# Attention with all products on 128 rows of weights, both parts of V side by side, in a hybrid encoder kernel

## The chip, the cores and the metric

The kernel runs on one core of one Trainium2 chip. The metric is device time in microseconds (us) of one execution; lower is better. The time before is the median of three runs, 1886.88 us (1886.74 to 1887.07).

## The reference, cut to what matters

The program is a two-layer encoder on 512 tokens of width 1024. Layer 0 has a pooling and state-space mixer, layer 1 has the attention that the change is about. The tokens form a grid of 8 rows by 64 columns; each of 16 heads (64 channels) lets a token see all 8 rows and 16 columns around its own.

```python
def neighborhood_attention(h, w_qkv, rpb, w_out):
    qkv = (h @ w_qkv).reshape(bsz, rows, GRID_W, 3, N_HEADS, HEAD_DIM)
    q = qkv[:, :, :, 0] * (HEAD_DIM ** -0.5)
    k = qkv[:, :, :, 1]
    v = qkv[:, :, :, 2]
    ...
    s = jnp.einsum('bqhd,biqjhd->bhqij', q_r, k_nb).astype(F32) + bias[None]
    p = jax.nn.softmax(s.reshape(bsz, N_HEADS, GRID_W, kh * KW), axis=-1)
    ...
    return jnp.einsum('bhqij,biqjhd->bqhd', p, v_nb)
    ...
    return o @ w_out

for layer in range(DEPTH):
    h = h + 0.5 * rms_norm(swiglu_ffn(rms_norm(h, g[0]), ...), g[1])
    h = h + rms_norm(mixer_or_attention(rms_norm(h, g[2])), g[3])
    h = h + 0.5 * rms_norm(swiglu_ffn(rms_norm(h, g[4]), ...), g[5])
```

## The kernel before

**Split numbers.** Each operand of a large product is stored as two parts, hi (its value in the 4-byte type fp32r) and lo (the rest). ScalarE writes hi by a copy, VectorE or GpSimd writes lo by a subtraction (`split_evac`, L391 to L405). A full product is three products in one sum: hi by hi, hi by lo, lo by hi (`mm3`, L179 to L183). Most lines of TensorE in the trace are therefore L181, L182 and L183; which product it is shows in the names of the tiles.

**The attention** (L766 to L981). Queries and keys are ordered by columns, so that a query tile of 128 tokens (16 columns by 8 rows) needs one contiguous set of 192 or 256 keys. A *unit* is one head and one of its four query tiles: 16 heads by 4 tiles are 64 units. Heads come in pairs `hp`; the two heads of a pair, `a` = 0 and 1, have their channels on partitions 0 to 63 and 64 to 127 of the projections' output.

- `evac_q` and `evac_k` (L786 to L805) split a pair's Q and K. Per head, tile `q0` or `q1` holds hi of the scaled Q on the head's own 64 partitions and lo on the other 64; tile `k0` or `k1` holds hi of K on both halves (L805 copies it across). One tile `k_lo` holds lo of K for both heads, each on its own half.
- `scores(u)` (L890): two products into the only bank `ps_qk`. L898 uses all 128 rows (hi and lo of Q against hi of K), L899 uses the head's 64 rows (hi of Q against lo of K). Then VectorE adds the bias, takes the row's extreme and writes `p` (L902), and ScalarE takes exp (L904).
- `normalize(u)` (L909): reciprocal and product on VectorE, L912 and L914.
- `transpose(u)` (L916): TensorE turns `p` (L922), and a split makes `pt_hi` and `pt_lo` (ScalarE L396, VectorE L397). For tiles 0 and 3 one of the two chunks has only 64 keys.
- `values(u)` (L931): per unit two chunks of keys, each an `mm3` of V's parts against the parts of P, 64 columns of weights and 128 columns moving. For tiles 0 and 3 one of the chunks has 64 rows. After tile 3 the 64x512 result is split into `oT`.

**What sets the order.** Each engine runs its instructions in the order in which the code issues them. The loop over `slot` (L946) runs the units in a software pipeline: in slot s stand the deferred VectorE work (`run_later`), normalize of unit s-1, values of unit s-5, transpose of unit s-3, scores of unit s, one step of `run_spread` (the splits of a new pair's Q and K), and 1.35 *fill steps* on average (`FILL_RATE`): pieces of the projections of V, Q and K of later heads, and in the last slots of the output projection. A fill step is six products of 512 columns or twelve of 256 (three of 512 in the output projection). After the loop the rest of the output projection runs, and the norm behind it uses `gpost`, a row of gains spread over all partitions.

Weights come by DMA from SyncE's queue (`w_raw`, two buffers). ScalarE makes `w_hi` (L124), and inside the loop GpSimd makes `w_lo` (L135). The same DMA queue brings the bias, 512 KB per head, two heads ahead, and `gpost`, which is loaded ahead of the attention (L769).

## Time and profile before

| | us |
|---|---|
| median of three runs | 1886.88 |
| the profiled execution, span of its instructions | 1884.6 |
| the profiled execution, its device time | 1886.41 |
| TensorE (PE) busy in the span | 1831.5 (97%) |
| weight loads (PEld) | 1639.3 (87%) |
| VectorE (DVE) | 1470.7 (78%) |
| ScalarE (ACT) | 925.7 (49%) |
| GpSimd (POOL) | 350.4 (19%) |
| the attention's loop, first to last score product | 1292.4 to 1485.1 |

The times of the timeline are counted from the span's start. A matmul's row has the time at which it starts and how long it is in the array; matmuls overlap, so that the distance between two starts, not the duration, is what one costs in a stream. The form `64*128 64x192` means weights of 64 rows by 128 columns, and an output of 192 columns; `128*64` has 128 rows and 64 columns. A wait names the engine that waits, the tile and line, and after the arrow what ended the wait; then the sum in us, how many times, and the longest.

### The profile page before, as it was taken

How to read it: one execution, taken by the hardware profiler on the slowest of the kernel's cores; microseconds unless marked ns; L12 is line 12 of the kernel's file. 1: busy time of each engine (PE TensorE's matmuls, PEld its weight loads, DVE VectorE, ACT ScalarE, POOL GpSimd, SP SyncE). 2: the span in 40 equal slices, each digit the busy share in tenths (PEclk: the TensorE clock that was granted, in tenths of full speed). 3: DMA queues.
4: the chain of work that ended last, by engine and by line, in shares of the span. 5: the costliest groups of instructions: out<-in, count | busy, mean ns of one | idle time of the engine just before them, and what ended most of it. 6: DMA issues, size and time to landing. Idle time of an engine off the chain costs nothing.

```text
span 1884.6 us, 31563 instructions
## 1 busy us (share of the span) xinstructions
PE 1831.5 (97%) x12368; PEld 1639.3 (87%) x12368; DVE 1470.7 (78%) x2380; ACT 925.7 (49%) x1749; POOL 350.4 (19%) x238
## 2 busy tenths in 40 slices
PE   7999999998899999999999999999999999999998
PEld 7887987787689999988999998888878789999886
DVE  6888989868779999844899996465565589999744
ACT  5254446354455444543644445355555465444532
POOL 2021322015011233200122320012222012322100
PEclk9999999999999999999999999999999999999999
DMA  6474346647432333332233324323222132333321
GB/s 196 128 224 165 110 137 194 202 132 256 161 125 79 101 112 102 107 107 78 94 109 102 103 89 135 101 80 122 90 93 99 62 106 96 102 106 102 123 96 62
DMA packets 82021, 225.48 MB, mean 120 GB/s; under 512 B 15792, under 2 KB 20048, under 8 KB 80848
## 3 DMA queue, kind: packets, MB, share of 16 engines
q1 hardware_dynamic: 70176, 197.80, 31.8%
q0 software_dynamic: 6960, 23.57, 4.1%
q10 hardware_dynamic: 4736, 2.10, 0.4%
q8 instruction: 97, 1.59, 0.4%
q14 instruction: 52, 0.43, 0.1%
HBM read 206.69 MB, written 18.84 MB: 120 GB/s over the span
## 4 chain that ended last, share of the span: by engine, by line
PE 62%; DVE 7%; ACT 3%; issue 1%; DMA 1%; DVEq 0%; ACTq 0%
PE ps_gu L183 10%; PE ps_gu L182 10%; PE ps_gu L181 10%; PE ps_A L183 3%; PE ps_A L182 3%; PE ps_A L181 3%; PE ps_B L182 3%; PE ps_B L181 3%; PE ps_B L183 3%; PE ps_f L181 3%; PE ps_f L182 2%; PE ps_f L183 2%; DVE w_lo L135 1%; PE ps_qk L899 1%; ACT junk L237 1%
## 5 line engine op out<-in xcount | busy, mean ns | idle before, releaser
L135 DVE TENSOR_TENSOR w_lo<-w_raw,w_hi 128x1024 fp32r<-128x1024 f32 x214 | 283.3, 1329 | 215.8 <-ACT w_hi L124 215.6
L124 ACT CAST w_hi<-w_raw 128x1024 fp32r<-128x1024 f32 (+1 forms) x313 | 262.9, 864 | 286.4 <-PE ps_A L183 71.3
L183 PE MATMUL ps_gu<-xT_hi,w_lo 128*128 128x256 f32 (+1 forms) x1008 | 307.5, 305 | 2.5 <-DVE w_lo L135 2.5
L183 PE MATMUL ps_gu<-xsum,w_lo 128*128 128x256 f32 x1088 | 308.2, 283 | 0.6 <-DVE w_lo L135 0.6
L182 PE MATMUL ps_gu<-xsum,w_hi 128*128 128x256 f32 x1088 | 307.8, 283 | 0.2 <-DVE xsum L518 0.2
L181 PE MATMUL ps_gu<-xsum,w_hi 128*128 128x256 f32 x1088 | 307.6, 283 | 0.0
L181 PE MATMUL ps_gu<-xT_hi,w_hi 128*128 128x256 f32 (+1 forms) x1008 | 304.9, 302 | 0.0
L182 PE MATMUL ps_gu<-xT_lo,w_hi 128*128 128x256 f32 (+1 forms) x1008 | 304.5, 302 | 0.0
L183 PEld LDWEIGHTS ps_gu<-xsum,w_lo 128*128 128x128 f32 x1088 | 208.6, 192 | 0.9 <-DVE w_lo L135 0.8
L182 PEld LDWEIGHTS ps_gu<-xsum,w_hi 128*128 128x128 f32 x1088 | 208.5, 192 | 0.4 <-DVE xsum L518 0.4
L181 PEld LDWEIGHTS ps_gu<-xsum,w_hi 128*128 128x128 f32 x1088 | 208.4, 192 | 0.0
L183 PEld LDWEIGHTS ps_gu<-xT_hi,w_lo 128*128 128x128 f32 x1008 | 190.4, 189 | 15.0 <-DVE w_lo L135 4.1
L181 PEld LDWEIGHTS ps_gu<-xT_hi,w_hi 128*128 128x128 f32 x1008 | 190.2, 189 | 8.5 <-issue 0.9
L182 PEld LDWEIGHTS ps_gu<-xT_lo,w_hi 128*128 128x128 f32 x1008 | 190.2, 189 | 7.3
L135 POOL TENSOR_TENSOR w_lo<-w_raw,w_hi 128x1024 fp32r<-128x1024 f32 x31 | 74.1, 2390 | 562.2 <-ACT w_hi L124 532.1
L109 POOL TENSOR_TENSOR w_u<-w_raw,w_s 128x512 f32<-128x512 f32 x64 | 112.2, 1754 | 354.9 <-ACT w_hi L124 196.3
L124 ACT CAST w_hi<-w_s 128x512 fp32r<-128x512 f32 x136 | 77.8, 622 | 197.3 <-DVE w_s L105 193.5
L105 DVE TENSOR_TENSOR w_s<-w_raw,w_u 128x1024 f32<-128x1024 f32 x68 | 145.8, 2144 | 2.3
L640 POOL TENSOR_TENSOR g<-g,m 128x1024 f32<-128x1024 f32 x34 | 94.6, 2782 | 244.9 <-DVE m L638 244.9
L181 PE MATMUL ps_B<-w_hi,gT 128*128 128x512 f32 x352 | 137.1, 389 | 1.6 <-DVE free L1264 1.6
L183 PE MATMUL ps_A<-w_hi,gT 128*128 128x512 f32 x352 | 137.1, 389 | 1.1 <-DVE gT L693 1.1
L181 PE MATMUL ps_A<-w_hi,gT 128*128 128x512 f32 x352 | 137.3, 390 | 0.0
(376 smaller groups left out, 4251.2 us busy)
## 6 DMA issues: line engine op xcount, KB each, us to landing
w_raw<-in_w_gu_dram SPq DMA_DIRECT2D x106, 512.0 KB, 3.4
w_raw<-in_w_dn_dram SPq DMA_DIRECT2D x88, 512.0 KB, 3.3
w_u<-in_w_gu_dram SPq DMA_DIRECT2D x70, 512.0 KB, 3.7
w_raw<-in_w_qk_dram SPq DMA_DIRECT2D x16, 512.0 KB, 3.3
bias<-in_att_bias_dram SPq DMA_DIRECT2D x16, 512.0 KB, 4.1
w_raw<-in_w_in_dram SPq DMA_DIRECT2D x8, 512.0 KB, 3.3
cm<-m_dram SPq DMA_DIRECT2D x4, 1024.0 KB, 8.7
w_raw<-in_w_ao_dram SPq DMA_DIRECT2D x8, 512.0 KB, 3.9
```

What stands on the lines that cost most here:

```text
L105: tt(out=blocks(s), in0=g[:, :HALF].unsqueeze(1).broadcast_to([P, 2, HALF]), in1=blocks(u)[:, :2], op=ALU.subtract)
L109: (h_engine or self.nc.gpsimd).tensor_tensor(out=z["h"], in0=g[:, HALF:], in1=z["s"][:, HALF:], op=ALU.add)
L124: self.nc.scalar.copy(hi[:, k:k + step], src[:, k:k + step])
L135: (engine or self.lo_engine).tensor_tensor(out=lo[:, :n], in0=src, in1=hi[:, :n].bitcast(F32), op=ALU.subtract)
L181: mm(ps, a[0], b[0], start=start, stop=False)
L182: mm(ps, a[0], b[1], start=False, stop=False)
L183: mm(ps, a[1], b[0], start=False, stop=stop)
L237: self.nc.scalar.activation(out=junk[:, :src.shape[-1]], in_=src, func=AF.Square, scale=scale, accum_out=out)
L640: nc.gpsimd.tensor_tensor(out=rows(f), in0=rows(f), in1=m, op=ALU.mult)
L899: nc.tensor.matmul(ps[:, :n], tq[rows], lo[rows], start=False, stop=True)
```

## The change

- **Scores.** K's lo gets the layout of its hi: a tile per head with lo on both halves. ScalarE's copy of hi across stays, and GpSimd copies lo across (`nc.gpsimd.tensor_copy`). Both products now use 128 rows. Lo of the second head of a pair lives in the buffer that `gpost` had; `gpost` is loaded after the loop.
- **V** is stored with hi and lo of a head side by side, 128 columns of weights: the upper 64 rows of the result are the sum with hi, the lower 64 the sum with lo.
- **P** lies in one buffer of eight chunks per part, four tiles by two; the unused halves of chunks 0 and 7 are zero, written once.
- **values** works after tiles 1 and 3 only. Two neighbouring chunks of two query tiles that need the same 128 keys are one product of 256 columns. After tile 3 ScalarE copies the lower half of the result out (`o_sum`), VectorE adds the upper half in the next slot, and the split follows one slot later than that. `run_later` runs what was there when it began, and a call made by it waits for the next slot.
- **Bias** is loaded per unit, four units ahead, in four buffers; `p` has four buffers where it had five.
- **After the loop** the output projection of token tile 3 starts with its first two weight tiles, and the last products of tiles 0 to 2 come behind them.
- **Elsewhere** a small constant of the mixer in layer 0, `edge`, is loaded in the mixer and not at the program's start.

```diff
         def run_later():
-            while later:
-                later.pop(0)()
+            now = later[:]
+            del later[:]
+            for f in now:
+                f()
...
-        def load_bias(head):
-            bias[head] = z["ap"].tile([P, 4, 256], F32, tag="bias", bufs=2, name="bias")
-            nc.sync.dma_start(bias[head], ins["att_bias"][head])
+        def load_bias(u):
+            if u < 64:
+                n = self.NKEY[u % 4]
+                bias[u] = z["ap"].tile([P, 256], F32, tag="bias", bufs=4, name="bias")[:, :n]
+                nc.sync.dma_start(bias[u], ins["att_bias"][u // 4, :, u % 4, :n])
...
         def evac_k(hp, ps):
-            k[hp] = [z["ap"].tile([P, SEQ], F32R, tag="k" + n, bufs=2, name="k" + n) for n in ("0", "1", "_lo")]
-            for a, x in enumerate(k[hp][:2]):
+            hi = [z["ap"].tile([P, SEQ], F32R, tag="k%d" % a, bufs=2, name="k%d" % a) for a in range(2)]
+            lo = [z["ap"].tile([P, SEQ], F32R, tag="k_lo", bufs=2, name="k_lo"), z["k_lo"][:, hp % 2]]
+            k[hp] = list(zip(hi, lo))
+            for a, x in enumerate(k[hp]):
                 own, other = own_other(a)
-                lo = []
-                self.split_evac(x[own], k[hp][2][own], ps[own], None, lo)
+                rest = []
+                self.split_evac(x[0][own], x[1][own], ps[own], None, rest)
                 yield
-                lo[0]()
-                nc.scalar.copy(x[other], x[own].bitcast(F32))
+                rest[0]()
+                nc.scalar.copy(x[0][other], x[0][own].bitcast(F32))
+                nc.gpsimd.tensor_copy(x[1][other], x[1][own].bitcast(F32))
...
-        vt = [ap.tile([P, TT, D], F32R, name=n) for n in ("v_hi", "v_lo")]
+        vt = ap.tile([P, TT, 16, 2, 64], F32R, name="v")
+        pt = [ap.tile([P, 8, P], F32R, name="pt" + n) for n in ("_hi", "_lo")]
+        for x in pt:
+            nc.scalar.mul(x[:64, 0], self.ident[:64], 0.0)
+            nc.scalar.mul(x[64:, 7], self.ident[64:], 0.0)
...
-            nc.tensor.matmul(ps[:, :n], tq, hi, start=True, stop=False)
-            nc.tensor.matmul(ps[:, :n], tq[rows], lo[rows], start=False, stop=True)
+            for i, x in enumerate(k[hp][a]):
+                nc.tensor.matmul(ps[:, :n], q[hp][a][:, t * P:(t + 1) * P], x[:, self.KEY0[t]:self.KEY0[t] + n],
+                                 start=i == 0, stop=i == 1)
...
         def values(u):
...
-            for c, (_, n, s, r) in enumerate(self.CHUNKS[t]):
-                self.mm3(o[:64, t * P:(t + 1) * P], [x[r:r + n, s, d0:d0 + 64] for x in vt],
-                         [x[r:r + n, c] for x in pt], c == 0, c == 1)
-            if t == 3:
-                hi, lo = (x[64 * a:64 * a + 64, hp, :].rearrange("p (r c) -> p r c", r=8) for x in oT)
-                self.split_evac(hi, lo, o[:64].rearrange("p (c r) -> p r c", r=8), None, later)
...
+            def product(s, *chunks):
+                n = len(chunks) * P
+                at = chunks[0] // 2 * P
+                for i, x in enumerate(pt):
+                    nc.tensor.matmul(o[:, at:at + n], head[:, s],
+                                     x[:, chunks[0]:chunks[-1] + 1].rearrange("p c n -> p (c n)"),
+                                     start=s == 1 and i == 0, stop=chunks[-1] == 7 and i == 1)
+            if t == 1:
+                product(1, 1, 2)
+                product(0, 0)
+                return
+            product(3, 5, 6)
+            product(2, 3, 4)
+            product(0, 7)
...
+            w = ap.tile([P, SEQ], F32, tag="o", bufs=1, name="o_sum")[64 * a:64 * a + 64]
+            nc.scalar.copy(w, o[64:])
+            def rest():
+                V.tensor_tensor(out=w, in0=o[:64], in1=w, op=ALU.add)
+                self.split_evac(hi, lo, by_row(w), None, later)
+            later.append(rest)
...
-        run_later()
+        while later:
+            run_later()
+        self.load_gpost(1, 3)
...
-        for _ in out_steps((0, 1, 2), (KT - 1,)):
-            pass
-        self.post_pair(0, 0, psA)
         for kt in range(KT):
             for _ in out_steps((3,), (kt,)):
                 pass
+            if kt == 1:
+                for _ in out_steps((0, 1, 2), (KT - 1,)):
+                    pass
+                self.post_pair(0, 0, psA)
```

On TensorE, near the loop's end: the last values of a slot, the two transposes and the scores of a 256-key unit before the change. `ps_o` is the result of the values, `ps_pt` the turned P, `ps_f` a fill product; the shape behind a name is that of the output.

```order
L181 MATMUL ps_o<-pt_hi,v_hi 64x128
L182 MATMUL ps_o<-pt_lo,v_hi 64x128
L183 MATMUL ps_o<-pt_hi,v_lo 64x128
L922 MATMUL ps_pt<-ident,p 128x128
L922 MATMUL ps_pt<-ident,p 64x128
L898 MATMUL ps_qk<-k_15462,q_15348 128x256
L899 MATMUL ps_qk<-k_lo,q_15348 128x256
L181 MATMUL ps_f<-w_hi,oT_hi 128x512
```

The same place after it, in the slot of the values of tile 1.

```order
L958 MATMUL ps_o<-pt_hi,v 128x256
L958 MATMUL ps_o<-pt_lo,v 128x256
L958 MATMUL ps_o<-pt_hi,v 128x128
L958 MATMUL ps_o<-pt_lo,v 128x128
L934 MATMUL ps_pt<-ident,p 128x128
L934 MATMUL ps_pt<-ident,p 64x128
L911 MATMUL ps_qk<-k_15324,q_15215 128x256
L911 MATMUL ps_qk<-k_lo,q_15215 128x256
L181 MATMUL ps_f<-w_hi,oT_hi 128x512
```

The values went from 24 products a head, of 64x128 each, to 10 of 128 output rows; the transposes and the number of score products stayed.

On VectorE, where a head ends in the last slots, before: two ISA rows are the reduction L902 and its accumulator.

```order
L902 ISA p,att_m<-ps_qk,bias 128x192
L902 ISA att_m 128x1
L397 TENSOR_TENSOR oT_lo<-ps_o,oT_hi 64x512
L397 TENSOR_TENSOR pt_lo<-ps_pt,pt_hi 128x256
L912 RECIPROCAL att_r<-att_s 128x1
L914 TENSOR_SCALAR p<-p,att_r 128x192
L902 ISA p,att_m<-ps_qk,bias 128x256
```

And after: the reduction is L915, reciprocal and product L924 and L926.

```order
L975 TENSOR_TENSOR o_sum<-ps_o,o_sum 64x512
L397 TENSOR_TENSOR pt_lo<-ps_pt,pt_hi 128x256
L924 RECIPROCAL att_r<-att_s 128x1
L926 TENSOR_SCALAR p<-p,att_r 128x192
L915 ISA p,att_m<-ps_qk,bias 128x256
L915 ISA att_m 128x1
L397 TENSOR_TENSOR oT_lo<-o_sum,oT_hi 64x512
```

The addition `o_sum` took the place of `oT_lo`, and `oT_lo` moved behind the next reduction.

On GpSimd, the last weights of the loop before:

```order
L135 TENSOR_TENSOR w_lo_15101<-w_raw_14848,w_hi_15100 128x1024
L135 TENSOR_TENSOR w_lo_15210<-w_raw_14963,w_hi_15209 128x1024
L135 TENSOR_TENSOR w_lo_15351<-w_raw_15104,w_hi_15350 128x1024
L135 TENSOR_TENSOR w_lo_15466<-w_raw_15213,w_hi_15465 128x1024
L135 TENSOR_TENSOR w_lo_16088<-w_raw_15928,w_hi_16087 128x1024
```

and after, the copies for the last pair of heads:

```order
L135 TENSOR_TENSOR w_lo_15218<-w_raw_14992,w_hi_15217 128x1024
L135 TENSOR_TENSOR w_lo_15328<-w_raw_15093,w_hi_15327 128x1024
L811 CAST k_lo_15325<-k_lo_15325 64x512
L811 CAST k_lo_13017<-k_lo_13017 64x512
L135 TENSOR_TENSOR w_lo_15902<-w_raw_15742,w_hi_15901 128x1024
```

Two copies of lo of K now stand on GpSimd for each pair, behind a `w_lo`.

## Rows read from the trace of the kernel before

**Rows 1.** The page: span, and the granted clock of TensorE in 40 slices.
```profile
span 1884.6 us, 31563 instructions
...
PEclk9999999999999999999999999999999999999999
```

**Rows 2.** Busy time by stretch in us, instructions in brackets; granted clock, DMA.
```profile
core 0: us, PE busy (x) PEld busy (x) DVE busy (x) ACT busy (x) POOL busy (x), PEclk, DMA share, GB/s
...
1350.00:1400.00 50.00, 50.00 (x331) 40.64 (x330) 29.86 (x97) 30.09 (x79) 12.02 (x6) 1.00 0.28 95
...
1470.00:1493.00 23.00, 23.00 (x152) 17.64 (x151) 13.71 (x52) 10.41 (x35) 0.00 (x0) 1.00 0.13 46
```

**Rows 3.** Waits of VectorE in the loop, 1292 to 1494 us.
```profile
DVE p L902 <- PE ps_qk L899: 53.4, 48, 2.7
DVE att_r L912 <- ACT p L904: 11.1, 25, 1.9
```

**Rows 4.** Timeline of TensorE at unit 0 (192 keys): start us, us.
```profile
1292.39 0.25 PE L898 MATMUL ps_qk<-k,q 128*128 128x192 f32 x1
1292.57 0.35 PE L899 MATMUL ps_qk<-k_lo,q 64*128 64x192 f32 x1
1292.86 0.38 PE L181 MATMUL ps_f<-w_hi,xT_hi 128*128 128x256 f32 x1
1293.08 0.28 PE L182 MATMUL ps_f<-w_lo,xT_hi 128*128 128x256 f32 x1
```

**Rows 5.** The same view at unit 2 (256 keys).
```profile
1297.88 0.38 PE L899 MATMUL ps_qk<-k_lo,q 64*128 64x256 f32 x1
...
1298.42 0.28 PE L182 MATMUL ps_f<-w_lo,xT_hi 128*128 128x256 f32 x1
1298.54 0.28 PE L183 MATMUL ps_f<-w_hi,xT_lo 128*128 128x256 f32 x1
```

**Rows 6.** The same view at the values of a tile 3.
```profile
1354.60 0.28 PE L183 MATMUL ps_f<-w_hi,xT_lo 128*128 128x256 f32 x1
1354.71 0.22 PE L181 MATMUL ps_o<-pt_hi,v_hi 128*64 128x128 f32 x1
...
1354.84 0.22 PE L183 MATMUL ps_o<-pt_hi,v_lo 128*64 128x128 f32 x1
1354.99 0.27 PE L181 MATMUL ps_o<-pt_hi,v_hi 64*64 64x128 f32 x1
1355.10 0.22 PE L182 MATMUL ps_o<-pt_lo,v_hi 64*64 64x128 f32 x1
...
1355.31 0.44 PE L922 MATMUL ps_pt<-ident,p 128*128 128x128 f32 x2
```

**Rows 7.** Timeline of the weight loads behind unit 0's scores.
```profile
1292.86 0.19 PEld L181 LDWEIGHTS ps_f<-w_hi,xT_hi 128*128 128x128 f32 x1
1292.96 0.19 PEld L182 LDWEIGHTS ps_f<-w_lo,xT_hi 128*128 128x128 f32 x1
1293.08 0.19 PEld L183 LDWEIGHTS ps_f<-w_hi,xT_lo 128*128 128x128 f32 x1
```

**Rows 8.** VectorE's groups in the loop: count, busy us, mean ns, idle before.
```profile
L397 DVE TENSOR_TENSOR oT_lo<-ps_o,oT_hi 64x512 fp32r<-64x512 f32 x16 | 10.9, 682 | 2.7 <-ACT oT_hi L396 2.4
```

**Rows 9.** Line L914 alone: duration in ns, least, median, longest.
```profile
L914 DVE TENSOR_SCALAR p<-p,att_r x64: 319/353/1124, 1296.6 to 1486.8; 128x192 f32<-128x192 f32 x32, 128x256 f32<-128x256 f32 x32
```

**Rows 10.** GpSimd's groups in the whole span: count, busy us, mean ns, idle before.
```profile
L135 POOL TENSOR_TENSOR w_lo<-w_raw,w_hi 128x1024 fp32r<-128x1024 f32 x31 | 74.1, 2390 | 562.2 <-ACT w_hi L124 532.1 <-PE ps_pt L922 20.8 <-PE ps_qk L899 9.3
...
L1485 POOL TENSOR_TENSOR pz<-pz 128x543 f32<-128x543 f32 x4 | 4.4, 1092 | 34.2 <-ACT pz L1479 34.2
```

**Rows 11.** Timeline at unit 56, the first of the last pair of heads.
```profile
1467.00 2.38 POOL L135 TENSOR_TENSOR w_lo<-w_raw,w_hi 128x1024 fp32r<-128x1024 f32 x1 [7.47 <-ACT w_hi L124]
...
1467.22 0.68 DVE L397 TENSOR_TENSOR k_lo<-ps_f,k 64x512 fp32r<-64x512 f32 x1
...
1468.64 0.35 PE L898 MATMUL ps_qk<-k,q 128*128 128x192 f32 x1
```

**Rows 12.** DMA issues: count, KB each, median us from issue to landing.
```profile
bias<-in_att_bias_dram SPq DMA_DIRECT2D x16, 512.0 KB, 4.1
...
gpost<-in_norm_g_dram SPq DMA_DIRECT2D x6, 512.0 KB, 5.6
```

More of the change, by code (lines that the diff above doesn't have):

```diff
@@ L812, in start @@
             z["ap"] = tc.alloc_tile_pool(name="attn", bufs=1)
-            load_bias(0)
-            load_bias(1)
+            z["k_lo"] = self.base.tile([P, 2, SEQ], F32R, tag="gpost", bufs=1, name="k_lo")
+            for u in range(4):
+                load_bias(u)
         def evac_first(i, ps):
@@ L847, in v_steps @@
             for b, ps in enumerate(pv):
-                hi, lo = (x[:, 2 * b:2 * b + 2, c * 256:(c + 1) * 256] for x in vt)
-                self.split_evac(hi, lo, ps.rearrange("p (s n) -> p s n", s=2), None, later)
+                hi, lo = (vt[:, 2 * b:2 * b + 2, 4 * c:4 * c + 4, i] for i in range(2))
+                self.split_evac(hi, lo, ps.rearrange("p (s h d) -> p s h d", s=2, h=4), None, later)
             self.W.done()
@@ L891, in scores @@
             hp, a, t = u // 8, u // 4 % 2, u % 4
-            rows, n = slice(64 * a, 64 * a + 64), self.NKEY[t]
+            n = self.NKEY[t]
             ps = self.bank("ps_qk")
@@ L905, in scores @@
             st[u] = p, s
-            if t == 3 and 2 * hp + a + 2 < 16:
-                load_bias(2 * hp + a + 2)
+            load_bias(u + 4)
         def normalize(u):
@@ L916, in transpose @@
         def transpose(u):
-            p, _ = st[u]
+            p, _ = st.pop(u)
             ps = self.bank("ps_pt")
-            pt = [ap.tile([P, 2, P], F32R, tag="pt" + n, bufs=2, name="pt" + n) for n in ("_hi", "_lo")]
-            ch = self.CHUNKS[u % 4]
+            t = u % 4
+            ch = self.CHUNKS[t]
             for c, (o, n, _, _) in enumerate(ch):
@@ L923, in transpose @@
             if ch[0][1] == ch[1][1]:
-                self.split_evac(pt[0], pt[1], ps[:, :256].rearrange("p (c n) -> p c n", c=2), None, later)
+                self.split_evac(*(x[:, 2 * t:2 * t + 2] for x in pt),
+                                ps[:, :256].rearrange("p (c n) -> p c n", c=2), None, later)
             else:
                 for c, (_, n, _, r) in enumerate(ch):
-                    self.split_evac(pt[0][r:r + n, c], pt[1][r:r + n, c], ps[:n, c * P:(c + 1) * P],
-                                    None, later)
@@ L929, in transpose @@
-            st[u] = pt
+                    self.split_evac(*(x[r:r + n, 2 * t + c] for x in pt), ps[:n, c * P:(c + 1) * P], None, later)
         def values(u):
             hp, a, t = u // 8, u // 4 % 2, u % 4
-            if t == 0:
-                st["o"] = self.bank("ps_o")
-            o = st["o"]
-            pt = st.pop(u)
-            d0 = (2 * hp + a) * 64
-            for c, (_, n, s, r) in enumerate(self.CHUNKS[t]):
-                self.mm3(o[:64, t * P:(t + 1) * P], [x[r:r + n, s, d0:d0 + 64] for x in vt],
-                         [x[r:r + n, c] for x in pt], c == 0, c == 1)
@@ L941, in values @@
-            if t == 3:
-                hi, lo = (x[64 * a:64 * a + 64, hp, :].rearrange("p (r c) -> p r c", r=8) for x in oT)
-                self.split_evac(hi, lo, o[:64].rearrange("p (c r) -> p r c", r=8), None, later)
+            if t == 1:
+                o = st["o"] = self.bank("ps_o")
+            elif t == 3:
+                o = st.pop("o")
+            else:
+                return
+            head = vt[:, :, 2 * hp + a].rearrange("p s i d -> p s (i d)")
+            def product(s, *chunks):
[5 more added lines that the diff above has]
+                                     start=s == 1 and i == 0, stop=chunks[-1] == 7 and i == 1)
@@ L1339, in mixer @@
         xh, xl = self.xT
-        edge, scol, bcol = self.mix_small
+        scol, bcol = self.mix_small
         con = {}
@@ L1356, in start @@
         def start():
-            nonlocal yp, y, yhl, sp, us
+            nonlocal yp, y, yhl, sp, us, edge
             yp = tc.alloc_tile_pool(name="mix_y", bufs=1)
@@ L1361, in start @@
             sp = tc.alloc_tile_pool(name="mix", bufs=1)
+            edge = sp.tile([P, 4, 16], F32, name="edge")
+            G.dma_start(edge, ins["pool_edge"].partition_broadcast(P))
             us = sp.tile([P, 32, 64], F32, name="us")
@@ L1666, in build @@
             self.mix_small = [self.base.tile([P, *n], F32, name="mix_" + k)
-                              for k, *n in (("edge", 4, 16), ("scol", 4), ("bcol", 4))]
+                              for k, *n in (("scol", 4), ("bcol", 4))]
             self.h = self.base.tile([P, TT, D], F32, name="h")
@@ L1687, in first_norm @@
         step(1)
[L1688 to L1689 removed]
+        scol, bcol = self.mix_small
         nc.gpsimd.dma_start(scol, self.ins["pool_sc"])
```

15 lines of the change are left out of this document (7 added, 8 removed).

## The prediction

> **What bounds the kernel now.** I read the page first, then the stretches of the attention, then who waits in it, and last the order of TensorE's starts. The granted clock is full in all 40 slices [rows 1], so no time hides in the clock. In the loop TensorE is busy in all of 50 us and all of 23 us of two stretches, while VectorE and ScalarE have 30 of 50 us and GpSimd 12 [rows 2]. VectorE waits for the score products, 53.4 us in 48 of the 64 units [rows 3]; TensorE hardly waits for it. So here the time is the sum of the distances between TensorE's starts, and I priced the change in these distances.
>
> In a stream with equal shapes, 256 columns come every 0.11 to 0.12 us [rows 4 to 6]; I take 0.117. Products of 128 columns on 64 columns of weights come every 0.06 us (0.13 for two steps) [rows 6]. A change between 128 and 64 rows breaks the stream. Of a 192-key unit without transposes ahead of it, L898 starts at 1292.39, L899 0.18 later, the next fill product 0.29 after that, and the one behind it 0.22 later [rows 4]: 0.69 us from L898 to the second fill product. In the values of tile 3 the step to 64 rows is 0.15 us in place of 0.06, the next 0.11, and the step back to the transposes 0.15 [rows 6].
>
> **The change part by part.**
>
> *Scores.* With 128 rows throughout, the same distance would be two score products and one fill product. A product of 192 columns would be about 0.09 by its columns, but loads of 128 columns of weights start no closer than 0.10 to 0.12 (0.22 for two) [rows 7], so 0.11. That is 0.11 + 0.11 + 0.117 = 0.34, and 0.35 saved. With 256 keys, L899 to the second fill product is 0.54 against 0.51 [rows 4, 5]; L898 to L899, which in rows 5 includes a wait, I take as 0.18 + 0.03. That is 0.75 against 0.35, and 0.40 saved. 32 x 0.35 + 32 x 0.40 = 24.0 us. By 0.09 for 192 columns it is 1.3 us more, by 0.12 for everything about 1 us less.
>
> *Values.* Tile 3 takes 0.71 us from the last fill product to the transposes, less that product's own step of 0.117: 0.59 [rows 6]. Tile 0 has the same two changes of rows, 0.59. Tiles 1 and 2 take 6 x 0.06 = 0.36 each. A head costs 1.90 us. After it, a head has six products of 256 columns and four of 128, all on 128 columns of weights: 6 x 0.117, and for the small ones between 0.06 (what they cost now on 64 columns) and 0.117; I take the load's 0.11 [rows 7]. That is 1.14 us, and 0.76 saved; 16 heads give 12.2 us, with ends at 11.7 and 15.4. Both parts together: 36.2 us off TensorE in the loop, 0.57 a unit.
>
> [...] The rows show loads of 128 rows that start 0.11 us apart with 0.19 us each [rows 7], under products of 128 rows. [...]
>
> *VectorE.* Per head one more operation of 64x512: `oT_lo` from PSUM takes 0.68 us now [rows 8]; the addition `o_sum` reads PSUM too and I give it the same, with `oT_lo` in SBUF no cheaper. 16 x 0.68 = 10.9 us, 0.17 a unit. ScalarE gets 16 more copies of that size behind VectorE's addition; it has 20 us free in 50 [rows 2], so no cost, and if that cover were gone exp would come later by a copy.
>
> *What of it VectorE gives back.* It is the next bound: only one bank holds scores, so TensorE can't write unit u+1 before L902 has read unit u. The 53.4 us that it waits for TensorE [rows 3] shrink by 36.2 and by 10.9, and 6.3 us are left. Over the whole loop it would just do, but the slack is uneven: in 64 - 48 = 16 units L902 finds its scores ready, VectorE is late already, and what is taken off TensorE there it can't use. That is at most 16 x (0.57 + 0.17) = 11.8 us, and at least 0, when the next longer slot makes up for it. I take 8, nearer the upper end: the late units stand at the heads' and pairs' starts, where the splits of Q and K pile up (unit 56 in [rows 11]), and a late unit passes its delay on.
>
> *GpSimd.* 16 copies of 64x512, of which four lie ahead of the loop. No such copy is in the trace; the nearest rows are an addition of 128x543 at 1.09 us and `w_lo` of 128x1024 at 2.39, half of which is 1.2 [rows 10]. I take 1.1, with ends at half of the first row, 0.5, and at the whole of the second, 2.39. Each stands behind a `w_lo` in GpSimd's queue. By the count of fill steps a pair's K is split in slots 12, 18, 30, 36, 42 and 54 for first use in 16, 24, 32, 40, 48 and 56: four slots or six ahead, but two for pairs 4 and 7. For pair 7 `w_lo` runs from 1467.00 to 1469.38, and unit 56 starts at 1468.64 [rows 11]: its second product would wait until about 1470.5, 2 us; but VectorE is late there by nearly as much, so 0.5 counts, and as much for pair 4. Further, L914 takes 0.35 us alone and up to 1.12 beside GpSimd [rows 9]; 12 copies cost VectorE at most 12 x 0.77 = 9.2 us, and I count 0.7 of it as seen by TensorE. Together 1.7 us, between 0 and 6.
>
> *Edits with no cost.* The zeros of P are four small operations ahead of the first V projection, in which ScalarE has time. `gpost` lands in 5.6 us [rows 12]; it is issued after the last scores, and five slots and some products lie ahead of its first use, so it is hidden; without them the norm waits up to 5.6 us. The bias is now 64 loads of a quarter of the size, each waiting on SyncE's queue for L902 of its unit; behind it wait weight loads, which have two buffers and four split tiles ahead. A whole head's bias lands in 4.1 us [rows 12], and four slots of some 2.6 us are its lead; if a weight load in front of it waits for a `w_lo` (2.39), the lead still holds. After the loop the chain from the last value to `oT_lo` grows from two operations to four, about 1.3 us more; two weight tiles of token tile 3, six products of 512 columns, each two steps of 0.117, or 1.4 us, now stand in front. Without them the wait is 1.1 us. The `edge` load leaves the start and goes to GpSimd's queue in the mixer, where GpSimd waits 34.2 us for its first work [rows 10]. All zero, with 1 us to either side.
>
> *Sum.* 36.2 - 8 - 1.7 = 26.5 us. The profiled execution has a span of 1884.6 [rows 1] and took 1886.41, within 0.5 of the median of 1886.88; I take the gain off the median: 1860.4, so 1860.
>
> **The rivals.**
> - *VectorE doesn't hold TensorE back.* For it: 53.4 us of waiting exceeds 47.1 of new demand. Against it: the 16 late units. Then 36.2 us go, 1850.7; with the cheaper ends of the products 1849.
> - *The chain of VectorE and ScalarE takes over.* If `L914` and the new `oT_lo`, whose two operands are in SBUF, run beside GpSimd often, demand is 36.2 + 10.9 + 9.2 = 56.3, 2.9 above the 53.4; with all of 11.8 for uneven slots and 3 for the copies TensorE gives back 17.7. The gain is 18.5 and the time 1868.
> - *The pauses don't come from the change of rows*, and each load waits anyway. Scores save nothing; a head's values cost 6 x (0.11 + 0.117) + 4 x (0.11 + 0.06) = 2.04 against 1.90, and the time is 1886.9 + 2 = 1889. [...] Against it: the value products of tiles 1 and 2 have the same operands as those of 0 and 3 and no pause.
> - *Slower: the scores wait for GpSimd's copies.* The second product of the first unit of each head needs a copy that stands behind a `w_lo`: 2.39 + 1.09 = 3.5 us for each of the 12 copies in the loop is 42 us, against 36.2 - 8 saved: 1886.9 + 14 = 1901. It turns to slower when a copy costs more than 28/12 = 2.4 us. Against it: four of six pairs have 4 slots or more to spare.
>
> **How the numbers follow.** The forecast, a gain between 21 and 33 us, has 0.66; no holding back 0.10; the chain of VectorE and ScalarE 0.15; pauses that stay 0.04; slower by the copies 0.05. The time is 1860, with its own range 1853 to 1866. The range 1849 to 1872 takes in the second case and the third to a gain of 15 us and leaves out the last two and the tails, about 0.2. A measurement of this kernel can tell 0.2%, 3.8 us, from no change: faster 0.66 + 0.10 + 0.15 = 0.91; the case of the pauses gives the same, 0.04; slower 0.05.
>
> **What would show it.** Right: the two products L911 start 0.11 to 0.12 apart, with no longer step behind them; a head's values are ten products with 1.1 to 1.2 us of steps; the loop is about 26 us shorter; VectorE's wait for scores falls from 53 to some 15 us, and TensorE has waits for `att_m` of about 8 us that it lacks now; GpSimd's copies take about 1.1 us. Wrong: steps of 0.18 to 0.3 us that remain around L911; waits of L911 for GpSimd at more pairs than two; waits for the bias or `gpost`; or TensorE with 15 us and more of waits in the loop.

## The result, and the profile after

The changed kernel takes 1860.04 us (median of four runs, 1858.23 to 1861.25), beside 1886.81 for the kernel before in the same comparison: a ratio of 0.9857, with a 95% interval of 0.984 to 0.9874. The forecast was 1860, with a range of 1849 to 1872. The total was right, but some of its terms were off and made up for each other; most of what follows is about that.

The profiled execution took 1858.23 us. First the page's span and busy times (share of the span, count), to be read against [rows 1]:

```profile
span 1856.5 us, 31301 instructions
PE 1796.5 (97%) x12144; PEld 1623.3 (87%) x12144; DVE 1491.7 (80%) x2396; ACT 944.5 (51%) x1769; POOL 360.7 (19%) x254
```

"Loop" below is the time from the start of the first score product to the start of the last one.

| us | before | after | change |
|---|---|---|---|
| ahead of the loop | 1292.4 | 1288.2 | -4.2 |
| loop | 192.75 | 169.32 | -23.4 |
| behind it | 399.5 | 399.0 | -0.5 |
| span | 1884.6 | 1856.5 | -28.1 |

Of the 4.2 us ahead of the loop 1.7 are the clock: from 20 us on, the sum of (1 - granted clock), explained below, is 6.8 us there before and 5.1 after. In the other runs it lies between 5.1 and 12.0, though what runs there is nearly the same program; so one fall of the clock more or less need not come from an edit.

**TensorE's steps.** The timeline of TensorE in the changed kernel (start, duration, operation; weights' rows x columns, then the output), at unit 0 with 192 keys and at the values of a tile 1:

```profile
1288.22 0.26 PE L911 MATMUL ps_qk<-k,q 128*128 128x192 f32 x1
1288.31 0.28 PE L911 MATMUL ps_qk<-k_lo,q 128*128 128x192 f32 x1
1288.43 0.30 PE L181 MATMUL ps_f<-w_hi,xT_hi 128*128 128x256 f32 x1
1288.56 0.28 PE L182 MATMUL ps_f<-w_lo,xT_hi 128*128 128x256 f32 x1
...
1339.10 0.28 PE L958 MATMUL ps_o<-pt_lo,v 128*128 128x256 f32 x1
1339.21 0.22 PE L958 MATMUL ps_o<-pt_hi,v 128*128 128x128 f32 x1
1339.28 0.28 PE L958 MATMUL ps_o<-pt_lo,v 128*128 128x128 f32 x1
1339.39 0.41 PE L934 MATMUL ps_pt<-ident,p 128*128 128x128 f32 x2
```

From the first score product to the second fill product it is 0.34 us, where [rows 4] had 0.69: the long steps behind the 64-row product are gone. Of two value products of 128 columns the first is followed by the second after 0.06 to 0.07 us, not after the 0.11 that the forecast took; behind the second, where a transpose follows, it is 0.11.

**Waits in the loop** (engine, tile and line <- what ended the wait: us in total, times, longest), after:

```profile
DVE p L915 <- PE ps_qk L911: 13.8, 19, 2.3
PEld ps_qk L911 <- DVE att_m L915: 7.4, 9, 2.3
PEld ps_qk L911 <- POOL k_lo L811: 2.4, 2, 1.3
PEld ps_qk L911 <- ACT k L810: 1.9, 1, 1.9
```

The same rows of TensorE before, which did not stand ahead:

```profile
PEld ps_qk L898 <- DVE att_m L902: 1.1, 2, 1.0
PEld ps_qk L898 <- ACT k L805: 0.2, 1, 0.2
```

VectorE's wait for scores fell from 53.4 [rows 3] to 13.8 us. TensorE's weight loads for the scores wait 11.7 us in place of 1.3 (its products wait in the same gaps, and are not counted again). The longest waits stand ahead of unit 2 (1.4, and 1.0 before), unit 17 (2.3), unit 41 (1.0), the second product of unit 32 (1.2), and both products of unit 56 (1.9 and 1.3).

**The clock.** The stretches of 1 us behind the wait of unit 17 (busy time of PE, PEld, DVE, ACT, POOL with counts, then the granted clock, the DMA share, GB/s), and TensorE's products there:

```profile
1333.00:1334.00 1.00, 0.00 (x0) 0.00 (x0) 0.82 (x2) 0.12 (x1) 0.98 (x1) 1.00 0.00 0
1334.00:1335.00 1.00, 0.70 (x3) 0.62 (x4) 1.00 (x4) 0.66 (x3) 0.00 (x0) 0.85 0.11 12
1335.00:1336.00 1.00, 1.00 (x4) 0.81 (x3) 0.90 (x5) 1.00 (x1) 0.00 (x0) 0.50 0.89 242
1336.00:1337.00 1.00, 1.00 (x4) 0.81 (x3) 0.97 (x1) 0.87 (x3) 0.00 (x0) 0.50 0.93 355
1337.00:1338.00 1.00, 1.00 (x4) 0.72 (x4) 0.88 (x4) 0.00 (x0) 0.00 (x0) 0.50 0.46 136
1338.00:1339.00 1.00, 1.00 (x6) 0.83 (x5) 0.00 (x0) 0.00 (x0) 0.00 (x0) 0.94 0.03 9
```

```profile
1334.30 0.39 PE L911 MATMUL ps_qk<-k,q 128*128 128x256 f32 x1 [2.10 <-DVE att_m L915]
...
1336.29 0.63 PE L182 MATMUL ps_f<-xT_lo,w_hi 128*128 128x512 f32 x1
1336.71 0.63 PE L183 MATMUL ps_f<-xT_hi,w_lo 128*128 128x512 f32 x1
...
1338.28 0.39 PE L181 MATMUL ps_f<-xT_hi,w_hi 128*128 128x512 f32 x1
1338.51 0.40 PE L182 MATMUL ps_f<-xT_lo,w_hi 128*128 128x512 f32 x1
```

Right behind a wait of 2.3 us the granted clock of TensorE was 0.50, and products of 512 columns came every 0.42 us in place of 0.23. The same happens from 1444.0 on, behind the waits of unit 56. Before, the loop has no such stretch; over the whole of it the granted clock is 1.00:

```profile
1292.00:1485.00 193.00, 192.25 (x1223) 154.06 (x1221) 115.79 (x388) 111.84 (x295) 47.85 (x20) 1.00 0.28 95
```

What the clock took is the sum of (1 - granted clock) over stretches of 1 us, 1.7 us for each of the two, 3.4 together.

So a loop splits into waits, clock, and the rest, which I call steps: before 1.3 + 0 + 191.4, after 11.7 + 3.4 + 154.2. TensorE's steps are 37.2 us shorter, and 13.8 us of that went back: 10.4 to waits, 3.4 to the clock. There is one trace of each kernel, so a single fall of the clock, 1.7 us of loop, may come and go without any edit; where a reading below hangs on one, the text says so.

### The profile page after: what moved, and what is told of

It is laid out like the page before. It is cut to its first block, busy times and chain, and to the rows that moved or that the text cites. A ratio compares the mean times of both kernels' runs of the same rounds, so it can differ in the third digit from the quotient of the medians.

```text
span 1856.5 us, 31301 instructions
## 1 busy us (share of the span) xinstructions
PE 1796.5 (97%) x12144; PEld 1623.3 (87%) x12144; DVE 1491.7 (80%) x2396; ACT 944.5 (51%) x1769; POOL 360.7 (19%) x254
## 4 chain that ended last, share of the span: by engine, by line
PE 58%; DVE 9%; ACT 4%; issue 2%; DMA 1%; POOL 0%; DVEq 0%; ACTq 0%; POOLq 0%
PE ps_gu L183 10%; PE ps_gu L182 10%; PE ps_gu L181 10%; PE ps_A L181 3%; PE ps_A L183 3%; PE ps_A L182 3%; PE ps_B L183 3%; PE ps_B L182 3%; PE ps_B L181 3%; PE ps_f L181 2%; PE ps_f L183 2%; DVE w_lo L135 2%; PE ps_f L182 2%; ACT junk L237 1%; DVE xsum L518 1%
```

## The experiments

All runs in one table, split in the same way (us; waits are those of the weight loads for scores). The last column is the ratio of the time to the kernel before, whose median lay between 1884.8 and 1886.8 in these comparisons; so runs are compared by ratio or by loop.

| run | loop | waits | clock | steps | time | ratio (95%) |
|---|---|---|---|---|---|---|
| before | 192.75 | 1.3 | 0 | 191.4 | 1886.8 | |
| after | 169.32 | 11.7 | 3.4 | 154.2 | 1860.0 | 0.9857 (0.9840 to 0.9874) |
| e1_rows | 174.75 | 4.7 | 1.7 | 168.3 | 1868.0 | 0.9909 (0.9893 to 0.9924) |
| e8_values | 181.99 | 4.8 | 0 | 177.2 | 1872.5 | 0.9922 (0.9906 to 0.9939) |
| e3_by_row | 165.51 | 9.6 | 1.7 | 154.2 | 1853.6 | 0.9832 (0.9816 to 0.9848) |
| e6_lazy | 164.56 | 8.5 | 1.7 | 154.4 | 1854.0 | 0.9827 (0.9812 to 0.9842) |
| e2_no_copy | 168.08 | 11.7 | 1.7 | 154.7 | 1856.2 | 0.9844 (0.9830 to 0.9858) |
| e10_twice | 173.08 | 13.9 | 5.1 | 154.1 | 1862.5 | 0.9875 (0.9859 to 0.9892) |
| e12_busy | 167.07 | 9.2 | 0 | 157.9 | 1856.6 | 0.9845 (0.9832 to 0.9858) |
| e7_mended | 162.55 | 6.4 | 1.7 | 154.4 | 1850.7 | 0.9809 (0.9793 to 0.9825) |
| e11_half | 163.22 | 6.5 | 3.4 | 153.3 | 1852.1 | 0.9822 (0.9806 to 0.9839) |
| e5_banks | 163.81 | 5.0 | 1.7 | 157.1 | 1862.6 | 0.9873 (0.9854 to 0.9892) |
| e9_banks2 | 180.58 | 2.3 | 3.4 | 174.9 | 1869.9 | 0.9917 (0.9902 to 0.9931) |
| e4_edge | 192.74 | 1.3 | 0 | 191.4 | 1883.4 | 0.9985 (0.9977 to 0.9994) |

The loop is a sharper measure than the time: e4 leaves it untouched and has 192.74 beside 192.75, while the whole time moves by some us from run to run, mostly ahead of the loop.

### Is the change of rows the cause, and what are scores and values worth?

e1_rows, on the kernel before:

```diff
-            nc.tensor.matmul(ps[:, :n], tq[rows], lo[rows], start=False, stop=True)
+            nc.tensor.matmul(ps[:, :n], tq, lo, start=False, stop=True)
```

> The kernel before with one line changed: the second score product takes all 128 rows of q and of k_lo. The other half of k_lo holds lo of the pair's other head, so a product of lo of Q with that head's lo of K is added; no copy on GpSimd is made. Theory (the pauses come from the change between 128 and 64 rows): L898 to L899 falls from 0.18 to 0.11 us, no longer step behind L899, 24.0 us off TensorE in the scores; of it VectorE, late in 16 units by up to 0.38 each, holds back 0 to 6, so the time is 1863 to 1869. Rival (each load waits anyway, whatever the rows): 1886 to 1888 and steps of 0.18 and more around L899 remain.

One line gives 18.0 us of loop. Steps fell by 23.1 us, where the forecast had 24.0 for the scores. The timeline of its unit 0:

```profile
1290.14 0.25 PE L898 MATMUL ps_qk<-k,q 128*128 128x192 f32 x1
1290.23 0.28 PE L899 MATMUL ps_qk<-k_lo,q 128*128 128x192 f32 x1
1290.34 0.30 PE L181 MATMUL ps_f<-w_hi,xT_hi 128*128 128x256 f32 x1
1290.48 0.28 PE L182 MATMUL ps_f<-w_lo,xT_hi 128*128 128x256 f32 x1
```

The products, their columns and the engines around them are those of [rows 4]; only the rows of one operand changed, and the steps fell from 0.18, 0.29 and 0.22 to 0.09, 0.11 and 0.14. So the pause belongs to the 64-row product. That it is the change of rows, and not the 64 rows by themselves, shows in the line of the kernel before that comes next in [rows 6]:

```profile
1355.16 0.22 PE L183 MATMUL ps_o<-pt_hi,v_lo 64*64 64x128 f32 x1
```

It starts 0.06 us behind the 64-row product ahead of it, as the 128-row products there do; only the steps next to a change are 0.11 and 0.15. The rival, by which each load of weights waits whatever the rows, would have left the time at 1886 to 1888; these rows and the 1868.0 us speak against it.

e8_values, on the changed kernel (with one k_lo tile per pair as in e2):

```diff
-                nc.tensor.matmul(ps[:, :n], q[hp][a][:, t * P:(t + 1) * P], x[:, self.KEY0[t]:self.KEY0[t] + n],
+                r = slice(64 * a * i, 128 - 64 * (1 - a) * i)
+                nc.tensor.matmul(ps[:, :n], q[hp][a][r, t * P:(t + 1) * P], x[r, self.KEY0[t]:self.KEY0[t] + n],
```

> The changed kernel with the scores of before: the second score product takes the head's 64 rows, one k_lo tile per pair, no GpSimd copies. What is left of the change is the values, the bias and the rest. Steps of TensorE: 12 to 13 us less than before. Theory A (the loss is VectorE's, late only because TensorE has become faster): with TensorE slower again nothing is held back, the values keep 11 us and more, and the loop is 192.7 - 11 = 180 to 182. Theory B (the new work of the values, o_sum and the split from SBUF, holds TensorE by itself): the loop is 184 to 187.

181.99 is in the range of theory A, but not by its account: the values' steps are 14.2 us, more than the 12 to 13 expected, and 3.5 of them go to waits, where theory A had nothing held back. Steps add up (23.1 + 14.2 = 37.3, both together 37.2), loops do not: 18.0 + 10.8 = 28.8, but both together without the copies (e2) give 24.7. Of the 4.1 us that are missing, 3.5 are waits that appear only when TensorE has both gains; the clock has no part in it, since it took 1.7 us in e1 alone and 1.7 in e2.

### What holds TensorE back?

e3_by_row, on the changed kernel (`by_row0` is the same view of a tile that already lies in oT's order):

```diff
-            w = ap.tile([P, SEQ], F32, tag="o", bufs=1, name="o_sum")[64 * a:64 * a + 64]
-            nc.scalar.copy(w, o[64:])
+            w = by_row0(ap.tile([P, SEQ], F32, tag="o", bufs=1, name="o_sum")[64 * a:64 * a + 64])
+            nc.scalar.copy(w, by_row(o[64:]))
...
-                V.tensor_tensor(out=w, in0=o[:64], in1=w, op=ALU.add)
-                self.split_evac(hi, lo, by_row(w), None, later)
+                V.tensor_tensor(out=w, in0=by_row(o[:64]), in1=w, op=ALU.add)
+                self.split_evac(hi, lo, w, None, later)
```

> The changed kernel with o_sum stored in the order of oT: ScalarE's copy and VectorE's addition read PSUM in steps of eight elements, and the split reads SBUF without steps. Theory A (VectorE and ScalarE read SBUF in steps of 32 bytes at half the pace that they have from PSUM): oT_hi falls from 1.20 to about 0.6 us and oT_lo from 1.30 to about 0.7, 0.6 us a head on each engine; of the 10 us on VectorE a third to a half reaches TensorE, so 1855 to 1857. Theory B (oT_lo is long because GpSimd shares VectorE's way to SBUF): oT_lo stays above 1.1 us and the time at 1859 to 1861.

The groups by line (operation, shapes, count | busy us, mean ns | idle before), of the changed kernel and then of e3:

```profile
L397 DVE TENSOR_TENSOR oT_lo<-o_sum,oT_hi 64x512 fp32r<-64x512 f32 x14 | 18.2, 1303 | 2.1 <-ACT oT_hi L396 1.8
L396 ACT CAST oT_hi<-o_sum 64x512 fp32r<-64x512 f32 x14 | 16.9, 1204 | 0.7 <-DVE o_sum L975 0.2
L972 ACT COPY o_sum<-ps_o 64x512 f32<-64x512 f32 x15 | 8.7, 583 | 4.9 <-PE ps_o L958 4.6
```

```profile
L397 DVE TENSOR_TENSOR oT_lo<-o_sum,oT_hi 64x512 fp32r<-64x512 f32 x14 | 12.9, 922 | 0.6 <-ACT oT_hi L396 0.4
L396 ACT CAST oT_hi<-o_sum 64x512 fp32r<-64x512 f32 x14 | 8.7, 619 | 0.8 <-DVE o_sum L976 0.2
L973 ACT COPY o_sum<-ps_o 64x512 f32<-64x512 f32 x15 | 8.7, 582 | 4.9 <-PE ps_o L958 4.6
```

With steps of 32 bytes through SBUF a read took twice as long (1204 against 619 ns); with the same steps through PSUM it took no longer (582 against 583). `oT_lo` fell less than expected, to 922 on the mean. Twelve of the 14 take 0.68 to 0.69 us, as this one does:

```profile
1336.62 0.68 DVE L397 TENSOR_TENSOR oT_lo<-o_sum,oT_hi 64x512 fp32r<-64x512 f32 x1
```

The other two, at 1324.68 and 1391.66, take 2.36, and GpSimd works beside them for 2.29 of it. In the changed kernel the twelve take 1.09 to 1.21 and the two 2.16, GpSimd beside them for 2.09; its copies there took 1.30 and 1.29 us, the other ten of the loop 0.60 to 0.61. In VectorE's operations of 64x512 with an operand in PSUM nothing of the kind shows: before, `k_lo` took 0.68 us beside GpSimd [rows 11], and 0.69 without it, at 1469.53. So theory B has a part too, in two heads. The loop lost 3.8 us, 2.1 of waits and 1.7 of clock: theory A, and a time 1.4 us below its range. The 1.7 are the drop behind unit 56, where e3 waits as long as the changed kernel does, so they are not shown to be the edit's.

e6_lazy, on the changed kernel (each pending split now carries its pair):

```diff
-            while u % 8 == 0 and spread:
+            while u % 8 == 0 and spread and spread[0][0] <= hp:
                 run_spread()
```

> The changed kernel, but at a pair's first unit only that pair's pending splits are forced; before, all pending ones were, and at units 16 and 40 these are the Q of the pair after. Theory A (VectorE is late there because of the forced splits, which stand behind ScalarE's w_hi): TensorE's waits ahead of units 17 and 41, 2.3 and 1.0 us, shrink below 0.5 each and the loop is 2 to 3 us shorter, 166.3 to 167.3. Theory B (the same work comes one slot later and holds TensorE there): the loop stays at 168.5 to 169.5.

164.56, better than theory A had it: the waits ahead of units 17 and 41 are gone (3.2 us), and the drop of the clock behind unit 17 with them (1.7). In the changed kernel VectorE waited 1.80 us at unit 17 for a split of Q that nobody needed for eight units, since ScalarE had a `w_hi` of 1.03 us, the new copy `o_sum` of 0.58 and a `pt_hi` of 0.37 ahead of it; at unit 41 the same three stood there. So ScalarE's new copies, which the prediction counted as free, are part of these two waits.

e2_no_copy, on the changed kernel:

```diff
-            lo = [z["ap"].tile([P, SEQ], F32R, tag="k_lo", bufs=2, name="k_lo"), z["k_lo"][:, hp % 2]]
-            k[hp] = list(zip(hi, lo))
+            lo = z["ap"].tile([P, SEQ], F32R, tag="k_lo", bufs=2, name="k_lo")
+            k[hp] = [(x, lo) for x in hi]
...
-                nc.gpsimd.tensor_copy(x[1][other], x[1][own].bitcast(F32))
```

> The changed kernel without GpSimd's copies: one k_lo tile for both heads of a pair, all its 128 rows used in the second product, so the other head's lo of K times lo of Q takes the place of the own head's. Theory A (the copies cost TensorE what its waits for k_lo show, 2.1 us as PE and 2.4 as weight loads, and GpSimd's 11 us beside VectorE): 3 to 5 us less than the changed kernel's 1860.0, and no slot of 4 us and more at units 16 and 17. Theory B (VectorE and ScalarE, which split K and Q there anyway, are late by as much): 1858.5 to 1860.

Its waits of TensorE in the loop:

```profile
PEld ps_qk L908 <- DVE att_m L912: 7.0, 8, 2.3
PEld ps_qk L908 <- DVE k_lo L397: 2.8, 2, 1.4
PEld ps_qk L908 <- ACT k L810: 1.9, 1, 1.9
```

The sum is 11.7 as before; the place of GpSimd's copy is taken by VectorE's split, which was late by as much. Theory B holds for the waits. The 1.2 us of loop that went are within the one drop of the clock (1.7) that this run lacks, behind unit 17, although the wait there is as long as it was, 2.3 us; so they are not shown to be the copies'. The time, 1856.2, lies in theory A's range all the same, but of the 3.4 us between the two traces' spans 2.0 lie ahead of the loop, where the starts scatter by more than that.

e10_twice makes each copy twice:

```diff
-                nc.gpsimd.tensor_copy(x[1][other], x[1][own].bitcast(F32))
+                for _ in range(2):
+                    nc.gpsimd.tensor_copy(x[1][other], x[1][own].bitcast(F32))
```

> The changed kernel with each of GpSimd's copies of k_lo made twice, 0.69 us more for each. Theory A (the copies are on the path at pairs 4 and 7 only, where L911 waited for them 2.1 us in two waits): two units wait 0.7 us longer each, the loop is 170.5 to 171. [...] Theory C (hidden behind VectorE and ScalarE): 169.3.

Its row of waits, and a stretch of 2 us behind the wait of unit 32:

```profile
PEld ps_qk L912 <- POOL k_lo L812: 3.8, 2, 1.9
```

```profile
1381.00:1383.00 2.00, 2.00 (x8) 1.57 (x7) 0.99 (x4) 1.40 (x4) 0.20 (x1) 0.50 0.40 124
```

Two waits for GpSimd, 1.4 us more together, as theory A said: only pairs 4 and 7 are touched. But the loop is 173.08, 2 us more than A allowed, yet less than half of the 8.3 us that 12 copies on the path would add (12 x 0.69): the other waits of the table, for VectorE, grew by 0.8 us, and the clock fell a third time, behind the wait of unit 32, which grew from 1.2 to 1.8 us. That the longer wait brought this fall is likely, but one trace does not show it.

e5_banks and e9_banks2 give the scores a second bank, the first on the changed kernel at the cost of a bank of `ps_o`, the second on e7_mended at the cost of one of `ps_pt`:

```diff
-        self.new_psum(ps_f=3, ps_qk=1, ps_pt=2, ps_o=2)
+        self.new_psum(ps_f=3, ps_qk=2, ps_pt=2, ps_o=1)
```

```diff
-        self.new_psum(ps_f=3, ps_qk=1, ps_pt=2, ps_o=2)
+        self.new_psum(ps_f=3, ps_qk=2, ps_pt=1, ps_o=2)
```

> The changed kernel with two banks for scores and one for the values' sums, in place of one and two. Theory A (one bank ties TensorE to VectorE: it may not write unit u+1 before VectorE has read unit u): the waits of L911 for att_m, 7.5 us in the loop, mostly go and the loop falls from 169.3 us to 163 to 166. Theory B (the work of VectorE and ScalarE at the starts of heads is itself too long, a second bank only moves the wait to the transposes and splits behind it, or the single ps_o bank makes a new one): the loop stays within 1.5 us of 169.3.

> The three mended edits with two banks for scores and one for the transposes; the values' sums keep two, so the banks of the stage after the loop lie where they lay. Theory A (the second score bank frees TensorE, and only the moved ps_o bank made the stage after the loop 8.5 us longer in the run with one ps_o bank): waits of L911 for att_m, 2.3 us, go, from the last score to the end it is 394 to 396 us again, the loop 160 to 162.5. Theory B (one transpose bank is a new tie: transposes of unit u+1 wait for VectorE's split of unit u): new waits of L934 take what L911's lose, and the loop is 162.5 to 167.

In e5 no wait of L911 for `att_m` is left in the loop, which falls to 163.81: theory A, the single bank is the tie. (Among its steps in the table are 2.7 us of other waits, for the splits of V and for `p`.) But the stage behind the loop became 8.5 us longer. A wait there, and the stretch around it with a granted clock of 0.83 over 20 us, which is 3.4 us:

```profile
PE ps_B L181 <- ACT junk L237: 5.2, 1, 5.2
```

```profile
1470.00:1490.00 20.00, 14.76 (x57) 11.80 (x57) 5.70 (x11) 4.63 (x10) 0.00 (x0) 0.83 0.27 94
```

The next stage's first bank is now one that the norm still reads. In e9, where `ps_o` kept its two banks, the stage behind the loop has 399.5 us as before, but its loop is 18 us longer than e7's:

```profile
PE ps_pt L932 <- DVE att_r L922: 13.3, 16, 1.9
PEld ps_pt L932 <- DVE pt_lo L397: 5.0, 6, 1.2
```

Of these 18.3 us, 17.0 lie in the loop and stand among its steps in the table. With one bank the transposes wait for VectorE's split of the unit before (the wait is put down to the reciprocal `att_r`, which follows that split on VectorE). Theory B, and four times what I had allowed for it: where each kind of bank is tight, moving one moves the tie.

### Does a wait cost the clock?

e12_busy, on the changed kernel, ahead of the score products:

```diff
+            if u in (17, 56):
+                st["idle"] = self.bank("ps_o")
+            for _ in range({17: 6, 56: 6, 57: 4}.get(u, 0)):
+                x = k[hp - (u == 56)][0][0]
+                nc.tensor.matmul(st["idle"], x[:, :P], x, start=True, stop=True)
```

> The changed kernel with 16 products of 512 columns added whose result nothing uses: six ahead of the scores of unit 17, six ahead of unit 56, four ahead of unit 57, where TensorE waited 2.3, 1.9 and 1.3 us. At 0.232 us each they are 3.7 us of work within 5.5 us of waiting. In the changed kernel the granted clock was 0.5 for 3.4 us each from 1334.7 and 1444.0 us on, right behind these waits, and products of 512 columns came every 0.427 us there. Theory A (the waits bring the clock down, and the clock costs as much again): with the waits filled the clock stays at 1.0 and the loop is 169.3 - 3.4 = 165.5 to 166.5, though TensorE does more. Theory B (the clock falls for another reason): it falls again and the loop is 169 to 170. Theory C (the added products stand in the way): 171 to 173.

Stretches of 3 us behind the two places, with the changed kernel first and e12 second:

```profile
1335.00:1338.00 3.00, 3.00 (x9) 2.34 (x8) 2.75 (x9) 1.87 (x4) 0.00 (x0) 0.50 0.76 244
...
1444.00:1447.00 3.00, 3.00 (x11) 2.41 (x10) 2.70 (x9) 2.77 (x7) 0.25 (x1) 0.50 0.64 224
```

```profile
1335.00:1338.00 3.00, 2.89 (x13) 2.41 (x14) 2.76 (x9) 2.64 (x6) 0.00 (x0) 1.00 0.65 205
...
1444.00:1447.00 3.00, 3.00 (x19) 2.55 (x18) 2.59 (x8) 2.27 (x6) 0.00 (x0) 1.00 0.56 180
```

The clock stayed full throughout the loop, and the loop is 2.3 us shorter than without the 16 useless products. The split shows the 3.7 us of them in the steps (157.9 against 154.2), 2.5 taken from the waits and 3.4 from the clock. This is what theory A's cause would give. Left unfilled, waits of that length had a fall behind them in three of four traces at unit 17 (not in e2) and in six of seven at unit 56 (not in e3), so a trace with neither fall speaks for that cause without proving it. The loop is 0.6 longer than theory A said, because the four products ahead of unit 57 were misplaced: the wait of 1.3 us that I meant is that of unit 56's second product, and it stayed. As a version it is no gain over e6, which removes a wait instead of filling it.

### The edits together

e7_mended joins e2, e3 and e6 and loads `gpost` ahead of the attention again. e11_half joins e3 and e6, keeps the copies, and at a pair's first unit forces only its first head's splits (`done` counts the parts of a pending split that have run):

```diff
-            while u % 8 == 0 and spread and spread[0][0] <= hp:
+            while u % 4 == 0 and any(x[0] <= hp and done[x[1]] < 2 + a for x in spread):
                 run_spread()
```

> Three edits together on the changed kernel: no GpSimd copies (alone 1.2 us off the loop), o_sum in the order of oT (alone 3.8 off), only the own pair's splits forced; and gpost is loaded ahead of the attention again, since its buffer is free. Theory A (each relieves another place): the loop falls by 6 to 8 us to 161.3 to 163.3, and the time to about 1852. Theory B (they relieve the same late units): by 4 to 5 us, as o_sum alone.

> The changed kernel (with GpSimd's copies and the late gpost) with o_sum in the order of oT and, at a pair's first unit, only the first head's splits of that pair forced; those of its second head wait until that head's first unit. Theory A (what still waits at units 32, 56 and 57, 4.3 us in the run of the three edits, is VectorE's and ScalarE's work for the second head): these waits fall by 1 to 2.5 us, the loop is 160 to 162, and where the wait is short enough the clock stays up, for 1.7 more. Theory B (the first head's own K is late there): the loop is 162.5 to 164.

e7 has the lowest time: 1850.67 us, 0.9809 of the kernel before (0.9793 to 0.9825), and its interval lies below that of the changed kernel. Its loop, 162.55, is theory A. Singly the three edits gave 1.2 + 3.8 + 4.8 = 9.8, together 6.8: e2's share was the drop of the clock behind unit 17, which e6 removes as well, and the drop behind unit 56, which e3 lacks, is back in e7; both differences are falls of the clock. Like e1 and e2, e7 multiplies lo of Q by lo of the other head's K, where the changed kernel has the own head's; e11 keeps the own head's, at 1852.1. e11's loop is 163.22, theory B by its waits: those at units 32 and 56 stay at 4.1 us, so they are the first head's own K. Behind unit 56 its clock was low twice as long (3.4 us lost), with the same waits as in e7; without that the loop would be 161.5, so its length alone does not tell the theories apart.

### The start

e4_edge is the kernel before with the load moved:

```diff
+            edge = sp.tile([P, 4, 16], F32, name="edge")
+            G.dma_start(edge, ins["pool_edge"].partition_broadcast(P))
...
-        nc.gpsimd.dma_start(edge, self.ins["pool_edge"].partition_broadcast(P))
```

> The kernel before with only the load of edge moved from the program's start into the mixer. Theory A (this load delays the first weights: the first ps_p product starts at 13.8 us before and at 11.3 in the changed kernel): the start is 2 to 3 us earlier, with what the mixer gives 2.5 to 4.2 us in all, so 1882.7 to 1884.3. Theory B (the start differs from run to run, and the 4.2 us ahead of the loop have nothing to do with edge): 1886.5 to 1887.

0.9985 (0.9977 to 0.9994), 1.1 to 4.3 us: theory A by the time. The first 14 us of the kernel before, of the changed one, and of e4, in the DMA view (queue: packets, MB, share of 16 engines; then issues: KB each, us to landing):

```profile
q0 software_dynamic: 128, 0.09, 11.2%
...
gcol<-in_g_col_dram SPq DMA_DIRECT2D x1, 48.0 KB, 8.6
mix_edge<-in_pool_edge_dram POOLq DMA_DIRECT2D x1, 32.0 KB, 7.7
```

```profile
q0 software_dynamic: 96, 0.05, 1.7%
...
gcol<-in_g_col_dram SPq DMA_DIRECT2D x1, 48.0 KB, 6.0
```

```profile
gcol<-in_g_col_dram SPq DMA_DIRECT2D x1, 48.0 KB, 7.3
```

A load of 32 KB that is spread over all partitions took about 9.5% of the DMA engines' time while the first inputs came in; without it `gcol` lands 2.6 us sooner in the changed kernel and 1.3 in e4, and the first projection starts at 11.3 and 12.6 us where it started at 13.8. So e4's own start is 1.2 us earlier, less than theory A's 2 to 3. Ahead of that projection TensorE waited 2.33 us before and 0.56 in e4. Over all runs that start is at 13.3 and 13.8 with the load, and at 11.1 to 12.6 without. The loop's own start scatters more (1290.1 and 1292.4 with it, 1286.3 to 1291.7 without), so the size within a single trace is not to be trusted.

## Why the prediction was right, step by step

- **Scores, 24.0 us of steps:** 23.1 measured (e1). Right, and so is the cause, the change of rows.
- **Values, 12.2 us, ends 11.7 and 15.4:** 14.2 (e8). The term was mis-sized: I took 0.11 us, a load of weights, for every 128-column product; half of them come after 0.06, so that a head's ten products take 1.05 us and not 1.14. And tile 0, which I set equal to tile 3's 0.59, took 0.65 before. The end at 15.4, worked out with 0.06, was nearer.
- **VectorE's new work, 10.9 us:** the addition was as forecast (682 ns), but "`oT_lo` in SBUF no cheaper" missed that it would be dearer, 1303 in place of 682 ns, another 10 us on VectorE and as much on ScalarE. The row that I took had its steps in PSUM.
- **Held back, 8 us, and 1.7 for the copies:** waits grew by 10.4 and the clock took 3.4, so 13.8 against 9.7. The mechanism (one bank, late at the starts of pairs and heads) is what e5 and e6 show; ScalarE's copies, put at nothing, have a part in two of the waits (e6). Missing was the clock: "no time hides in the clock" was read from a kernel whose TensorE hardly waited in the loop, and the change brought the waits. It was also read too far: a 9 in [rows 1] is 90% or more, and ahead of the loop, behind the first 20 us, the clock took 6.8 us of that kernel. Of the copies, pairs 4 and 7 were the right ones, but their price in waits is zero (e2), not 1.0. The copies took 0.72 us, within 0.5 to 2.39.
- **Edits at no cost:** `gpost`, the bias, the zeros and the tail were free; the part behind the loop changed by 0.5 us, and no wait for a bias or `gpost` is among those in the loop. `edge` was not: 2.8 us by e4's ratio (1.1 to 4.3). I had priced where the load went, not what it left.
- **The sum:** forecast 36.2 - 9.7 = 26.5. Measured 37.2 - 13.8 = 23.4 in the loop, 0.5 behind it and about 2.8 ahead, 26.7, beside 26.8 between the medians. That this closes to 0.1 us is chance, since e4's interval is wider than that. And the total hit 1860 by luck: too little given back and nothing for the start cancelled. Without that 2.8 the time would be near 1863, still within the range.
- **The rivals:** "VectorE doesn't hold back" fell with 11.7 us of waits; "pauses not from the rows" fell with e1; "slower by the copies" with two waits of 2.4 us in all and with e2. "VectorE and ScalarE take over" had a grain of truth, in `oT_lo` and `oT_hi`, but the loop still moved with TensorE's steps.

## What to carry to other kernels

Where an engine that was never waiting is made faster, price its new waits twice: their length, and the clock that TensorE may lose behind them; a wait of about 2 us cost nothing or 1.7 us more here, once 3.4. Measure gains as steps, waits and clock of the stretch, since here steps added up between the parts of the change (23.1 + 14.2 beside 37.2) and the loops didn't (28.8 beside 24.7). Before a result is moved from PSUM to SBUF, look at the steps in which the next engine will read it: here `oT_lo` went from 0.68 to 1.30 us.
